# Down-projection of a ConvGLU layer: weight sums by accumulating DRAM transfers, activations put one combination at a time

## The chip, the cores and the metric

The kernel runs on one core of a Trainium2 chip. The metric is the device time of one execution in microseconds; the median of three runs of the kernel before is 2883.06 us (2882.86 to 2888.05). A profile is one further execution, taken by the hardware profiler.

In the profile PE is TensorE (products), PEld its weight loads, DVE is VectorE, ACT ScalarE, POOL GpSimd and SP the engine that only issues transfers. Each engine works through its own instructions in order; semaphores order the engines against each other.

## The reference

One layer of a streaming encoder, for 512 prompt frames and 64 sample frames: two recurrent mixers with their projections, then a ConvGLU feed-forward block, then a norm. What matters here is the feed-forward block (`D_MODEL` 2048, `D_FF` 5632, float32):

```python
def conv_ffn(h, st, w_up, ffn_conv_w, ffn_conv_b, w_down):
    gate, val = jnp.split(h @ w_up, 2, axis=-1)
    gate_c, new_st = causal_dwconv(gate, st, ffn_conv_w)
    act = jax.nn.silu(gate_c + ffn_conv_b) * val
    return act @ w_down, new_st
...
    f, s_f = conv_ffn(h, ffn_s[l], w_up[l], ffn_conv_w[l], ffn_conv_b[l], w_down[l])
    x = x + g2 * f
```

## The kernel before

**Products.** Frames stand on the free axis in two halves of 288 columns (256 prompt and 32 sample frames; 290 in the up-projection). Every float32 operand is split into a high and a low part (`hi` on ACT, `lo = x - hi` on DVE), and each product is three matmuls: hi by hi, hi by lo, lo by hi. Both projections of the feed-forward block use a fast two-by-two scheme with seven products in place of eight: the weight is cut into four blocks a11, a12, a21, a22, the activation into b11, b12, b21, b22, and the seven products (`c` = 0 to 6) take single blocks or sums of them, on both sides. The seven weights of a block are a11, s2 = s1 + a11, s1 = a21 + a22, a12, a11 + a21, s2 + a12 and a22.

**Up-projection** (`up`). 44 units `t`, each with seven products of 24 matmuls. `up_prep` runs two products ahead: it splits the weight of product `n + 2` into one of three buffers `wh`/`wl` (L1320, L1321), makes the weight sums on DVE (L1331 s1, L1340 s2, L1350, L1355) and issues the loads of the next unit's blocks (L1314, four of 512 KB, in SP's order a21, a22, a11, then two stores of the last unit's activation, then a12). There are six raw buffers, so a load waits until DVE has split what stood there. `up_out` takes the products out of three PSUM banks x, y and z; product `c` adds to bank x, y, z, x, y, z, y for c = 0 to 6. So y is read after c = 1, after c = 4 (L1396) and after c = 6, and each read stands between two products that write to it. At the end of a unit the gate goes into the convolution's buffer `cb` (L1409, L1410), POOL copies two columns into the new state `fs` (L1413, L1414), and in the next unit DVE convolves (L1423, `up_conv`), POOL puts the old state into `cb` (L1418, `up_state`), and the activation of the unit goes to DRAM (`actd`, L1431).

**Down-projection** (`down`). Activation tiles 0 and 1 (`FIRST`) are multiplied in the plain way first; the last four are left to `final`, which also norms and stores. The 38 between form 19 pairs `j`, in `GROUPS` of 3, 4, 4, 4 and 4 pairs; a group has four blocks `q` of output columns, and a block seven products. One product of a four-pair group has 24 matmuls, so a block has 168.

* *Weights.* Per block, `down_load` brings the four raw blocks (L1517, 512 KB each, 384 KB in the first group), `down_prep` makes four sums on DVE (`down_first` L1535, then L1552, L1562, L1567) and seven splits (L1541 on ACT, L1542 on DVE), two products ahead.
* *Activations.* `pair_load` brings both tiles of a pair into staging buffers, `down_pair` makes the seven combinations, each put into a slot as high and low part (L1224 on ACT, L1225 on DVE), with four differences on DVE (L1497, L1500, L1501, L1505). The four pairs of the next group are made at the products (q, c) = (2, 0), (3, 1), (3, 3) and (3, 5), a whole pair at a time. A slot is free once PE has done the last block's product with it.
* *Sums out.* `down_out` adds each product to accumulators in SBUF (L1607 from x and y, L1605 from z). x and y are two rotating PSUM tiles, so the next block's products wait for the sums out of the block before.
* *Staging.* Activation and residual loads share four buffers (`stage`: the convolution's `cb`, `ca` and two `v`), among them the loads of activations 0 and 1 at the start (L1478, split at L1484 and L1485).
* *End of a column block* (`down_finish`): load the residual `xd` (L1615), add `e0` (L1618), scale (L1622), add the residual (L1624).

The order on each engine comes from the program's order and a scheduler that may move an instruction ahead of others; `issue_after(ins)` keeps instructions behind `ins` on its engine.

Of the kernel before, what the change touches and what calls it, by code (L numbers as in the profile page):

```python
# [53 lines left out]
FIRST, NDOWN, GROUPS = 2, 19, (3, 4, 4, 4, 4)  # L54

# [46 lines left out]
class Kern:  # L102
# [530 lines left out]
    def raw_late(self):  # L633

        pool, tag = self.raws[self.n_raw % N_RAW]
        self.n_raw += 1
        return pool.tile([P, 1024], F32, tag=tag, name=self.name("raw"))
# [778 lines left out]
    def up_state(self, t):  # L1416

        self.nc.gpsimd.tensor_copy(self.cb[:, 514:516], self.vmap["st_ffn"].rearrange("p (i t) -> p t i", i=2)[:, t])  # L1418

# [18 lines left out]
    def up(self):  # L1438
# [49 lines left out]
    def pair_load(self, j):  # L1488
        return [self.act_load(FIRST + j + half * NDOWN) for half in range(2)]

    def down_pair(self, j, raws):

        V = self.nc.vector
        (b11, b12), (b21, b22) = [(r[:, 0], r[:, 1]) for r in raws]
        put = lambda c, b: self.put(c, j, b, None, HT)
        put(B11, b11)
        V.tensor_tensor(b11, b11, b12, op=ALU.subtract)  # L1497
# [4 lines left out]
        put(T2, b12)  # L1502
        put(T3, t)
        put(B21, b21)
        V.scalar_tensor_tensor(b21, b12, -1.0, b21, op0=ALU.mult, op1=ALU.subtract)  # L1505
        put(B22, b22)
        put(T4, b21)

# [11 lines left out]
    def down_load(self, step, names):  # L1520
        g, q = step
        for n in names:
            row, half = {"a11": (0, 0), "a12": (0, 1), "a21": (1, 0), "a22": (1, 1)}[n]
            k0, k1 = self.down_rows(g, half)
            m = (8 * row + 2 * q) * P
            self.a[g, q, n] = self.down_raw(self.i["w_down"][0, k0 * P:k1 * P, m:m + 256].rearrange("(k p) n -> p k n", p=P))

    def down_sum(self, step, c):
        g, q = step
        n = GROUPS[g]  # L1530
        return self.ua.tile([P, 1024], F32, tag=f"s{c}", name=self.name("s"))[:, :n * 256].rearrange("p (k n) -> p k n", k=n)

    def down_first(self, step):
        s1 = self.a[(*step, "s1")] = self.down_sum(step, 1)
        self.nc.vector.tensor_tensor(s1, self.a[(*step, "a21")], self.a[(*step, "a22")], op=ALU.add)  # L1535
# [9 lines left out]
    def down_prep(self, step, c, following):  # L1545

        V, a = self.nc.vector, self.a
        g = lambda n: a[(*step, n)]
        if c == 0:
            w = self.down_split(g("a11"))  # L1550
            s2 = a[(*step, "s2")] = self.down_sum(step, 2)
            V.tensor_tensor(s2, g("s1"), g("a11"), op=ALU.add)  # L1552
        elif c == 1:
            w = self.down_split(g("s2"))
        elif c == 2:
            w = self.down_split(g("s1"))
            if following:
                self.down_load(following, ("a21", "a22"))
        elif c == 3:
            w = self.down_split(g("a12"))  # L1560
        elif c == 4:
            V.tensor_tensor(g("a21"), g("a11"), g("a21"), op=ALU.add)  # L1562
            w = self.down_split(g("a21"))
            if following:
                self.down_load(following, ("a11", "a12"))
        elif c == 5:
            V.tensor_tensor(g("s2"), g("a12"), g("s2"), op=ALU.add)  # L1567
            w = self.down_split(g("s2"))
        else:
            w = self.down_split(g("a22"))  # L1570
            if following:
                self.down_first(following)
        a[(*step, "w", c)] = w
# [35 lines left out]
    def down_finish(self, row, h, q):  # L1609

        nc, t = self.nc, self.acc[row, h][q]
        xt = self.stage()
# [3 lines left out]
        if row + h:  # L1616
            yield
            nc.vector.tensor_tensor(t, t, self.e0[q], op=ALU.add)  # L1618
# [7 lines left out]
    def down(self):  # L1626
# [5 lines left out]
        self.places = firsts = take(2 * FIRST)  # L1632
        firsts = list(firsts)
        acts = [self.act_split(self.act_load(k)) for k in range(FIRST)]
# [8 lines left out]
        self.places += free + firsts  # L1643
# [5 lines left out]
        blocks = [b for b, c in steps if c == 0] + [None]  # L1649
        prep = lambda n: self.down_prep(*steps[n], blocks[n // 7 + 1]) if n < len(steps) else None  # L1650
        raws = {0: self.pair_load(0)}
        for m0 in range(0, KD, 4):
            wh, wl = self.wtile(self.i["w_down"][0, :FIRST * P, m0 * P:(m0 + 4) * P].rearrange("(k p) n -> p k n", p=P))
            if m0 == 4:
                self.down_load(blocks[0], ("a21", "a22"))
            if m0 == 8:
                self.down_load(blocks[0], ("a11", "a12"))
                self.down_first(blocks[0])
# [8 lines left out]
            if j < GROUPS[0]:  # L1667
                raws[j + 1] = self.pair_load(j + 1)
                self.down_pair(j, raws.pop(j))
        for n in range(2):  # L1670
            prep(n)

        j, last, tasks = GROUPS[0], len(GROUPS) - 1, []
        acts, loads = [], list(range(NFF - 4, NFF))
        for n, (step, c) in enumerate(steps):
            g, q = step
            prep(n + 2)
            self.down_product(step, c)
            self.down_out(step, c)
            if q == 3:  # L1680
                self.places += [self.combos[c, sum(GROUPS[:g]) + i][2] for i in range(GROUPS[g])]
            if g < last and (q, c) in ((2, 0), (3, 1), (3, 3), (3, 5)):
                if j + 1 < NDOWN:
                    raws[j + 1] = self.pair_load(j + 1)
                self.down_pair(j, raws.pop(j))
                j += 1
            if g == last:
                if q == 0 and c < 4:
                    loads[c] = self.act_load(loads[c])
                if q == 0 and 1 < c < 6:  # L1690
                    acts.append(self.act_split(loads[c - 2]))
                if c > 2:
                    tasks.append(self.down_finish(*((0, 0), (1, 1), (0, 1), (1, 0))[c - 3], q))
                for t in tasks[:2]:
                    if next(t, self) is self:
                        tasks.remove(t)
        for t in tasks:
            for _ in t:
                pass
# [111 lines left out]
def layer_kernel(tc, i, o):  # L1811
    nc = tc.nc
    with ExitStack() as ctx:
# [14 lines left out]
        K.actd = [dp.tile([P, 2, HT], F32, name=f"actd{t}") for t in range(NFF)]  # L1828
        K.hp = pool(ctx, "hp", bufs=1)
# [138 lines left out]
```

## Time and profile before

| | us |
|---|---|
| median of three runs | 2883.06 |
| the profiled execution's own time | 2889.4 |
| its span, first to last instruction | 2887.6 |
| up-projection, last unit ends at about | 2331 |
| down-projection with the final part, about | 2331 to 2888 |

A row of the windows gives, for a stretch of the span, the busy time of each engine with its number of instructions, the clock that TensorE was granted (1.00 is full speed), the share of time in which the 16 DMA engines were busy, and what they moved. A row of the waits reads: engine, line and tile that waited, what it waited for, total us, times, longest. A row of the groups gives line, engine, operation, tiles and shapes, then the total busy time, the mean of one in ns, and the idle time ahead of them with what ended it. "PE g" or "PE bank" are matmuls into a PSUM tile of that name; L561 and L563 are the plain products of the kernel's helper `mm6`, L1373 to L1375 those of the up-projection, L1590 to L1592 those of the down-projection.

### The profile page before, as it was taken

The numbers are of one execution on the slowest core, as the hardware profiler recorded it, in microseconds if no ns is written. First come the engines' busy times: TensorE is split into PE (matmuls) and PEld (weight loads), VectorE is DVE, ScalarE is ACT, GpSimd is POOL, SyncE is SP. The second block draws the span as 40 slices with busy tenths as digits, with TensorE's granted clock in tenths as the row PEclk, the third lists the DMA queues.
The fourth block names the chain that finished last, engine by engine and source line by source line (L and its number), as shares of the span: only waits on it lengthen the run. The fifth ranks groups of instructions, "written<-read, shape, count | busy, mean of one in ns | idle before, by whom it ended". The sixth has DMA issues, their size and how long they took to land.

```text
span 2887.6 us, 52030 instructions
## 1 busy us (share of the span) xinstructions
PE 2814.7 (97%) x20596; PEld 2713.3 (94%) x20596; DVE 2304.2 (80%) x3742; ACT 1357.9 (47%) x2379; POOL 320.9 (11%) x587
## 2 busy tenths in 40 slices
PE   7999999999999999999999999999999989999998
PEld 3599999999999999999999999999999989999997
DVE  5788888777778787468887888888888879999995
ACT  7574566544333333255444444444444454434453
POOL 0005432233310001001000000000000000000000
PEclk9999999999999999999999999999999999999999
DMA  9875555555456449333333333333333344333451
GB/s 306 298 205 155 156 146 161 157 142 157 128 158 183 136 136 260 111 112 97 104 105 111 101 108 107 101 101 107 110 102 108 108 131 121 120 112 121 129 160 66
DMA packets 523465, 399.80 MB, mean 138 GB/s; under 512 B 50793, under 2 KB 456004, under 8 KB 523220
## 3 DMA queue, kind: packets, MB, share of 16 engines
q1 hardware_dynamic: 517796, 385.79, 45.4%
q0 software_dynamic: 5424, 10.68, 1.2%
q8 instruction: 162, 2.65, 0.4%
q14 instruction: 83, 0.68, 0.1%
HBM read 356.24 MB, written 40.13 MB: 137 GB/s over the span
## 4 chain that ended last, share of the span: by engine, by line
PE 84%; DVE 7%; DMA 4%; ACT 3%; issue 1%; SPq 0%; POOL 0%; ACTq 0%; DVEq 0%; POOLq 0%
PE g L561 18%; PE g L563 9%; PE g L1373 9%; PE g L1374 8%; PE g L1375 8%; PE bank L1374 3%; PE bank L1373 3%; PE bank L1375 3%; PE g L1590 3%; PE g L1592 3%; PE g L1591 3%; DVE acc L820 1%; PE bank L1592 1%; PE bank L162 1%; PE bank L1590 1%
## 5 line engine op out<-in xcount | busy, mean ns | idle before, releaser
L1373 PE MATMUL g<-slot,wh 128*128 128x290 f32 x1760 | 533.2, 303 | 2.7 <-ACT p L1385 2.7
L1374 PE MATMUL g<-slot,wh 128*128 128x290 f32 x1760 | 525.9, 299 | 0.0
L1375 PE MATMUL g<-slot,wl 128*128 128x290 f32 x1760 | 520.2, 296 | 0.0
L561 PE MATMUL g<-hh,wh 128*128 128x288 f32 x1984 | 450.0, 306 | 1.0 <-DVE gcb L989 1.0
L561 PE MATMUL g<-hl,wh 128*128 128x288 f32 x1984 | 432.1, 297 | 0.0
L563 PE MATMUL g<-hh,wl 128*128 128x288 f32 x1984 | 432.0, 298 | 0.0
L1320 ACT ACTIVATE wh<-raw 128x1024 fp32r<-128x1024 f32 x176 | 186.7, 1061 | 396.0 <-PE g L1374 391.7
L1373 PEld LDWEIGHTS g<-slot,wh 128*128 128x128 f32 x1760 | 331.1, 188 | 17.0 <-ACT p L1385 11.6
L1375 PEld LDWEIGHTS g<-slot,wl 128*128 128x128 f32 x1760 | 336.3, 191 | 0.0
L1374 PEld LDWEIGHTS g<-slot,wh 128*128 128x128 f32 x1760 | 334.8, 190 | 0.1
L561 PEld LDWEIGHTS g<-hh,wh 128*128 128x128 f32 x1984 | 319.1, 190 | 4.0 <-DVE gcb L989 1.2
L561 PEld LDWEIGHTS g<-hl,wh 128*128 128x128 f32 x1984 | 321.1, 189 | 0.3
L649 ACT ACTIVATE wh<-raw 128x1024 fp32r<-128x1024 f32 x163 | 172.6, 1059 | 315.5 <-PE g L561 278.6
L563 PEld LDWEIGHTS g<-hh,wl 128*128 128x128 f32 x1984 | 320.0, 189 | 0.2 <-issue 0.2
L650 DVE TENSOR_TENSOR wl<-raw,wh 128x1024 fp32r<-128x1024 f32 x163 | 198.9, 1222 | 55.2 <-ACT wh L649 53.5
L820 DVE SCALAR_TENSOR_TENSOR acc<-xr,ct,acc 128x512 f32<-128x512 f32 x322 | 230.0, 749 | 2.2 <-DMA xr<-in_w_ada_dram 2.2
L1590 PE MATMUL g<-slot,wh 128*128 128x288 f32 x760 | 225.4, 297 | 6.5 <-DVE slot L1607 6.5
L1321 DVE TENSOR_TENSOR wl<-raw,wh 128x1024 fp32r<-128x1024 f32 x176 | 214.7, 1220 | 18.8 <-ACT wh L1320 18.7
L1592 PE MATMUL g<-slot,wl 128*128 128x288 f32 x760 | 224.7, 296 | 0.0
L1591 PE MATMUL g<-slot,wh 128*128 128x288 f32 x760 | 224.5, 295 | 0.0
L1374 PE MATMUL bank<-slot,wh 128*128 128x290 f32 x704 | 210.1, 298 | 0.0
L1373 PE MATMUL bank<-slot,wh 128*128 128x290 f32 x704 | 209.4, 297 | 0.0
(410 smaller groups left out, 6085.0 us busy)
## 6 DMA issues: line engine op xcount, KB each, us to landing
raw<-in_w_up_dram SPq DMA_DIRECT2D x176, 512.0 KB, 4.1
raw<-in_w_in_dram SPq DMA_DIRECT2D x108, 512.0 KB, 4.0
xr<-in_w_ada_dram SPq DMA_DIRECT2D x86, 512.0 KB, 3.8
raw<-in_w_down_dram SPq DMA_DIRECT2D x76, 512.0 KB, 3.6
ax<-in_w_ada_dram SPq DMA_DIRECT2D x42, 512.0 KB, 3.9
hraw<-in_w_ada_dram SPq DMA_DIRECT2D x40, 512.0 KB, 9.1
raw<-in_w_out_dram SPq DMA_DIRECT2D x32, 512.0 KB, 4.3
raw<-actd SPq DMA_DIRECT2D x44, 288.0 KB, 3.2
```

What stands on the lines that cost most here:

```text
L561: T.matmul(ps[:, h if bank is None else bank, :n], wh, x[:, h, :n], start=f, stop=False)
L563: T.matmul(ps[:, h if bank is None else bank, :n], wl, ah[:, h, :n], start=False, stop=stop)
L650: nc.vector.tensor_tensor(lo[:, :n_], raw[:, :n_], hi[:, :n_].bitcast(F32), op=ALU.subtract)
L820: V.scalar_tensor_tensor(acc[s], w[:, k], col, acc[s], op0=ALU.mult, op1=ALU.add)
L1320: self.nc.scalar.activation(hi, src, AF.Copy)
L1321: self.nc.vector.tensor_tensor(lo, src, hi.bitcast(F32), op=ALU.subtract)
L1373: T.matmul(ps, wh[:, j], hi, start=(c < 3 and j == 0), stop=False, skip_group_check=True)
L1374: T.matmul(ps, wh[:, j], lo, start=False, stop=False, skip_group_check=True)
L1375: T.matmul(ps, wl[:, j], hi, start=False, stop=(j == NPAIR - 1), skip_group_check=True)
L1590: T.matmul(ps, wh[:, j, f], hi, start=(c < 3 and j == 0), stop=False, skip_group_check=True)
L1591: T.matmul(ps, wh[:, j, f], lo, start=False, stop=False, skip_group_check=True)
L1592: T.matmul(ps, wl[:, j, f], hi, start=False, stop=(j == n - 1), skip_group_check=True)
```

## The change

**Weight sums.** The four sums that a block needs become four arrays in DRAM per group, `ws[g]`: s1 = a21 + a22, s2 = s1 + a11, s3 = a11 + a21, s4 = s2 + a12, for all 1024 output columns at once. Each is made by POOL's transfers: a copy from DRAM to DRAM, then a transfer that adds to what stands there (`accum_op=add`). There are ten pieces (two tile rows of a group, or one, 1 MB or 0.5 MB) and eight transfers a piece, 80 in all, in two batches of five pieces, so that a transfer builds on the one five places back. `up` draws two of them in each unit, at c = 1 and c = 4, behind the copy of the old state (`issue_after(self.state_of)`). `down_load` then loads the weight of each product, a block of `w_down` or of `ws`, seven for a block in place of four, four products ahead of its split (`RAW_AHEAD`); the two buffers of the DVE sums join the raw buffers, eight in all. `down_prep` is left with the load and the split.

**Activations.** `down_pair` becomes a generator that yields after each put. `next_pairs` goes through the pairs of the next group; the loop draws one put in each product of block 2 and 0, 3, 4, 4, 3, 4, 3 in those of block 3. Activations 0 and 1 and the first group's pairs are loaded into free slots instead of staging buffers.

**End.** The steps of `down_finish` stand at fixed products (`events`): for the four accumulators of a column block the load at products 1 to 4, the scaling two products later and the residual one after that. The additions of `e0` stand at products 1 to 3. The last four activations are loaded and split one for each block of the last group.

```diff
+RAW_AHEAD = 4
...
     def up_state(self, t):
 
         self.nc.gpsimd.tensor_copy(self.cb[:, 514:516], self.vmap["st_ffn"].rearrange("p (i t) -> p t i", i=2)[:, t])
+        self.state_of = self.nc.cur_bb.bb.instructions[-1]
...
+        sums = self.down_sums()
         for n, (t, c) in enumerate(steps):
+            if c in (1, 4):
+                with self.tc.issue_after(self.state_of):
+                    next(sums, None)
...
-    def act_load(self, t):
-
-        raw = self.stage()
+    def act_load(self, t, place=None):
+
+        raw = self.slot(place, F32, HT) if place else self.stage()
         self.nc.sync.dma_start(raw, self.actd[t])
...
+    def next_pairs(self, pairs):
+
+        raws = [self.pair_load(pairs[0])]
+        yield
+        for n, j in enumerate(pairs):
+            if n + 1 < len(pairs):
+                raws.append(self.pair_load(pairs[n + 1]))
+            yield from self.down_pair(j, raws.pop(0))
...
+    def down_sums(self):
+
+        dma, add = self.nc.gpsimd.dma_start, ALU.add
+        pieces = [(g, k) for g in range(len(GROUPS)) for k in range(0, GROUPS[g], 2)]
+        for batch in (pieces[:5], pieces[5:]):
+            for op in range(8):
+                for g, k in batch:
+                    rows = slice(k * P, min(k + 2, GROUPS[g]) * P)
+                    a11, a12, a21, a22 = [self.down_block(g, *at)[rows] for at in ((0, 0), (0, 1), (1, 0), (1, 1))]
+                    s1, s2, s3, s4 = [w[rows] for w in self.ws[g]]
+                    to, of = ((s1, a21), (s1, a22), (s2, s1), (s2, a11), (s3, a11), (s3, a21), (s4, s2), (s4, a12))[op]
+                    if op % 2:
+                        dma(to, of, accum_op=add)
+                    else:
+                        dma(to, of)
+                    yield
+
+    def down_load(self, step, c):
         g, q = step
...
+        s1, s2, s3, s4 = self.ws[g]
+        src = (self.down_block(g, 0, 0), s2, s1, self.down_block(g, 0, 1), s3, s4, self.down_block(g, 1, 1))[c]
+        self.a[g, q, c] = self.down_raw(src[:, 2 * q * P:2 * (q + 1) * P].rearrange("(k p) n -> p k n", p=P))
...
-    def down_prep(self, step, c, following):
-
-        V, a = self.nc.vector, self.a
-        g = lambda n: a[(*step, n)]
-        if c == 0:
-            w = self.down_split(g("a11"))
-            s2 = a[(*step, "s2")] = self.down_sum(step, 2)
-            V.tensor_tensor(s2, g("s1"), g("a11"), op=ALU.add)
...
+    def down_prep(self, n):
+
+        steps = self.steps
+        if n + RAW_AHEAD < len(steps):
+            self.down_load(*steps[n + RAW_AHEAD])
+        if n < len(steps):
+            step, c = steps[n]
+            self.a[(*step, "w", c)] = self.down_split(self.a.pop((*step, c)))
...
+        self.raws += [(self.ua, "s1"), (self.ua, "s2")]
+        firsts = take(3 * FIRST)
+        loads = [self.act_load(k, firsts[k]) for k in range(FIRST)]
...
+        puts = {2: (1,) * 7, 3: (0, 3, 4, 4, 3, 4, 3)}
...
+        for q in range(4):
+            b = 7 * (4 * last + q)
+            for i, (row, h) in enumerate(((0, 0), (1, 1), (0, 1), (1, 0))):
+                f = self.down_finish(row, h, q)
+                for at in (1, 3, 4):
+                    events[b + i + at].append(lambda f=f: next(f, None))
...
-            if g < last and (q, c) in ((2, 0), (3, 1), (3, 3), (3, 5)):
-                if j + 1 < NDOWN:
-                    raws[j + 1] = self.pair_load(j + 1)
-                self.down_pair(j, raws.pop(j))
-                j += 1
...
+                for _ in range(puts[q][c] if q in puts else 0):
+                    next(pairs)
```

Where the instructions stand, at three places. First POOL in the middle of the up-projection, before: the two copies into `fs` and the copy of the old state into `cb`, unit after unit.

```order
L1413 COPY fs<-cb 128x2
L1414 COPY fs<-cb 128x2
L1418 COPY cb<-cols 128x2
L1413 COPY fs<-cb 128x2
L1414 COPY fs<-cb 128x2
```

The same place of the changed kernel. `ws` is an array of sums; L1561 is a copy, L1559 a transfer that adds; 16x16384 is a whole piece of another sum.

```order
L1419 COPY cb<-cols 128x2
L1561 DMA ws_186<-ws_185 16x16384
L1559 DMA ws_178<-in_w_down_dram 256x1024
L1414 COPY fs<-cb 128x2
L1415 COPY fs<-cb 128x2
L1419 COPY cb<-cols 128x2
```

Both transfers of a unit stand back to back behind the copy of the state, and ahead of the next unit's copies into `fs`.

Second ACT at the way from the up- to the down-projection, before: L1320 and L649 are weight splits (of the last unit, and of the plain products), L1409 to L1424 the last unit's gate and convolution, L1484 the splits of activations 0 and 1, L1224 puts.

```order
L1320 ACTIVATE wh_25433<-s_25267 128x1024
L1320 ACTIVATE wh_25462<-raw_25098 128x1024
L649 ACTIVATE wh_25597<-raw_25596 128x1024
L649 ACTIVATE wh_25693<-raw_25692 128x1024
L1484 ACTIVATE slot_25565<-raw_25563 128x576
L1409 ACTIVATE cb<-g_25395 128x512
L1410 ACTIVATE cb<-g_25395 128x64
L649 ACTIVATE wh_25793<-raw_25792 128x1024
L1412 ACTIVATE ca_25520<-cb,cols 128x578
L1424 ACTIVATE ca_25520<-ca_25520,cols 128x578
L1484 ACTIVATE slot_25559<-raw_25557 128x576
```

The same place of the changed kernel (L1321 and L650 are the weight splits, L1490 the splits of activations 0 and 1, L1386 and L1426 belong to the last two units):

```order
L1321 ACTIVATE wh_25431<-s_25335 128x1024
L1490 ACTIVATE slot_25661<-slot_25657 128x576
L1386 ACTIVATE p_3327_25465<-g_25435 128x290
L1321 ACTIVATE wh_25467<-raw_25269 128x1024
L1426 ACTIVATE ca_25397<-ca_25397,cols 128x578
L1490 ACTIVATE slot_25665<-slot_25659 128x576
L1321 ACTIVATE wh_25498<-raw_25196 128x1024
L1321 ACTIVATE wh_25533<-s_25367 128x1024
L1321 ACTIVATE wh_25562<-raw_25198 128x1024
L650 ACTIVATE wh_25705<-raw_25704 128x1024
```

Both splits moved from around the last convolution to ahead of the last unit's weight splits.

Third DVE at the end of the first group, before: L1542 are lo-splits of weights, L1605 and L1607 sums out of PSUM, L1225 puts, L1497, L1501 and L1505 differences of activations.

```order
L1605 TENSOR_TENSOR slot_25576<-bank_26554,slot_25576 128x288
L1225 TENSOR_TENSOR slot_26765<-raw_26680,slot_26765 128x288
L1225 TENSOR_TENSOR slot_26778<-t_3564_26772,slot_26778 128x288
L1497 TENSOR_TENSOR raw_26680<-raw_26680 128x288
L1225 TENSOR_TENSOR slot_26781<-raw_26682,slot_26781 128x288
L1501 SCALAR_TENSOR_TENSOR raw_26680<-raw_26680,raw_26682 128x288
L1225 TENSOR_TENSOR slot_26769<-raw_26680,slot_26769 128x288
L1505 SCALAR_TENSOR_TENSOR raw_26682<-raw_26680,raw_26682 128x288
L1225 TENSOR_TENSOR slot_26785<-raw_26682,slot_26785 128x288
L1542 TENSOR_TENSOR wl_26792<-s_26739,wh_26791 128x1024
```

The same place of the changed kernel (L1575 are lo-splits, L1617 and L1619 sums out, L1226 puts, L1509 and L1515 differences):

```order
L1617 TENSOR_TENSOR slot_25676<-bank_26652,slot_25676 128x288
L1226 TENSOR_TENSOR slot_26863<-raw_26778,slot_26863 128x288
L1509 SCALAR_TENSOR_TENSOR raw_26778<-raw_26778,raw_26780 128x288
L1575 TENSOR_TENSOR wl_26878<-raw_26714,wh_26877 128x1024
L1226 TENSOR_TENSOR slot_26869<-raw_26778,slot_26869 128x288
L1619 TENSOR_TENSOR slot_25680<-g_26650,slot_25680 128x576
L1515 SCALAR_TENSOR_TENSOR raw_26780<-raw_26778,raw_26780 128x288
L1226 TENSOR_TENSOR slot_26904<-raw_26780,slot_26904 128x288
L1575 TENSOR_TENSOR wl_26913<-raw_26753,wh_26912 128x1024
```

Five puts in a row became one or two between a lo-split and a sum out, and the lo-splits read raw loads where they read a DVE sum (`s`).

More of the change, by code (lines that the diff above doesn't have):

```diff
@@ L1687, in down @@
[L1687 to L1699, printed above, removed]
+            freed = lambda c: [self.combos[c, sum(GROUPS[:g]) + i][2] for i in range(GROUPS[g])]
@@ new lines, in down @@
+            if q == 3 and c > 0:
+                self.places += freed(c - 1)
+            if g < last:
+                if (q, c) == (1, 6):
+                    pairs = self.next_pairs(range(sum(GROUPS[:g + 1]), sum(GROUPS[:g + 2])))
+                    next(pairs)
+                for _ in range(puts[q][c] if q in puts else 0):
+                    next(pairs)
+            for f in events[n]:
+                f()
+            if q == 3 and c == 6:
+                next(pairs, None)
+                self.places += freed(c)
```

101 lines of the change are left out of this document (39 added, 62 removed).

## The prediction

> **What bounds the kernel now.** I read the page's first four parts, then the windows by stage, then the waits of the stage that changes, then one unit of the up-projection in order of time.
>
> ```profile
> PE 2814.7 (97%) x20596; PEld 2713.3 (94%) x20596; DVE 2304.2 (80%) x3742; ACT 1357.9 (47%) x2379; POOL 320.9 (11%) x587
> PE   7999999999999999999999999999999989999998
> PE 84%; DVE 7%; DMA 4%; ACT 3%; issue 1%; SPq 0%; POOL 0%; ACTq 0%; DVEq 0%; POOLq 0%
> ```
>
> TensorE is the bound. The change leaves the number of products as it is, so it can only take away, or add, time in which PE waits or runs at a lower clock.
>
> ```profile
> 1300.00:2300.00 1000.00, 996.88 (x7271) 982.23 (x7270) 819.01 (x1024) 451.73 (x548) 71.02 (x133) 1.00 0.36 105
> 2320.00:2400.00 80.00, 70.36 (x511) 69.59 (x510) 66.30 (x119) 45.41 (x97) 1.09 (x2) 0.94 0.45 135
> 2400.00:2800.00 400.00, 393.29 (x2948) 391.91 (x2948) 380.90 (x533) 187.46 (x284) 0.00 (x0) 1.00 0.43 127
> 2540.00:2620.00 80.00, 80.00 (x605) 80.00 (x605) 76.81 (x110) 34.28 (x46) 0.00 (x0) 1.00 0.40 122
> 2640.00:2660.00 20.00, 20.00 (x154) 20.00 (x153) 19.58 (x28) 7.48 (x9) 0.00 (x0) 1.00 0.31 97
> 2800.00:2820.00 20.00, 14.17 (x92) 13.87 (x91) 17.40 (x34) 9.37 (x22) 0.00 (x0) 0.83 0.43 135
> ```
>
> Columns: window, length, busy time and count of PE, PEld, DVE, ACT, POOL, granted clock, DMA share, GB/s. The first row is the up-projection: PE has 3 us of gaps in 1000, DMA stands at 0.36. The others are the down-projection. In its clean stretch (2540 to 2620) PE does 605 products in 80 us, 7.56 per us; DVE is 95% busy over 2400 to 2800.
>
> **What the change can take from the down-projection.** Products missing against the clean rate: (605 - 511) / 7.56 = 12.4 us at the way in; (5 x 605 - 2948) / 7.56 = 10.2 us in the 400 us of groups; (154 - 92) / 7.56 = 8.2 us where the final part begins. That is 30.8 us, the ceiling. Their causes, PE's waits from 2300 on:
>
> ```profile
> PE g L561 <- ACT slot L1484: 8.9, 1, 8.9
> PE g L1590 <- DVE slot L1607: 6.5, 5, 1.9
> PE bank L1787 <- DVE slot L1714: 5.8, 1, 5.8
> ```
>
> *Way in.* 8.9 us, the rest is the lower clock (0.94) after it. Activation 0 is loaded into a buffer that the last unit's convolution holds. The change loads it into slots that PE leaves with the last unit's first product, and the order on ACT has both splits (L1490 there) among that unit's weight splits. What is late next is the first weight split, which stands there already; I let 1 us stand: gain 11.
>
> *Groups.* DVE is late with its sums out of PSUM when a group changes. What it loses:
>
> ```profile
> L1542 DVE TENSOR_TENSOR wl<-raw,wh 128x1024 fp32r<-128x1024 f32 x64 | 78.0, 1218 | 0.6 <-ACT wh L1541 0.2
> L1607 DVE TENSOR_TENSOR slot<-g,slot 128x576 f32<-128x576 f32 x96 | 72.3, 753 | 4.1 <-PE g L1592 3.8
> L1225 DVE TENSOR_TENSOR slot<-raw,slot 128x288 fp32r<-128x288 f32 x114 | 49.6, 454 | 4.7 <-ACT slot L1224 4.7
> L1605 DVE TENSOR_TENSOR slot<-bank,slot 128x288 f32<-128x288 f32 x80 | 34.5, 452 | 5.1 <-PE bank L1592 4.8
> L1552 DVE TENSOR_TENSOR s<-s,raw 128x1024 f32<-128x1024 f32 x16 | 19.5, 1221 | 1.6 <-DMA raw<-in_w_down_dram 1.4
> L1562 DVE TENSOR_TENSOR raw<-raw,raw 128x1024 f32<-128x1024 f32 x16 | 19.5, 1218 | 0.0
> L1497 DVE TENSOR_TENSOR raw<-raw 128x288 f32<-128x288 f32 x19 | 8.6, 455 | 0.1
> ```
>
> DVE loses the four sums of each block (L1552 and L1562 are two of them): in 16 blocks of four tiles 64 x 1.22 = 78 us of some 450 us, and shorter ones in the four blocks of three tiles, so that it goes from 95% to about 77%. The last block of a group still holds seven lo-splits (7 x 1.22 = 8.5 us), its sums out (5 x 0.75 + 4 x 0.45 = 5.6), 21 puts (L1225) and 12 differences (L1497) at 0.45 (15): 29 us of DVE beside 168 products, 22.2 us. So DVE still falls behind there, but it now enters the block on time, has 4.9 us less to do in it than before, and its puts stand between the sums out instead of in three lumps. I take 8.5 of the 10.2 us; all or none of them are the bounds.
>
> *Final part.* The residual loads move two steps forward and no longer wait for a buffer at the end; the scaling and adding behind the last product stay. Of 8.2 us I take 5; bounds 0 and 8. Sum of the gains: **25 us**, between 11 and 31. The 60 more weight loads (seven for four in 20 blocks, 0.5 MB) add 30 MB to 450 us, 67 GB/s on 127; with four steps of 24 products (12.7 us) of lead they are covered by PE's own work; without it each load would cost the 4 us that it takes to land. The e0 additions and the residual's instructions only change places.
>
> **What it adds to the up-projection.** 80 transfers of up to 1 MB, DRAM to DRAM, two a unit. Order shows them back to back behind the copy of the state. What stands there (POOL, SP, DVE, PE in one unit; a unit is 900 us / 39 = 23 us by the last row):
>
> ```profile
> 1808.69 1.05 POOL L1418 COPY cb<-cols 128x2 f32<-128x2 f32 x1 [6.12 <-DVE ca L1423]
> ```
> ```profile
> 1809.72 0.37 SPq L1314 DMA_DIRECT2D raw<-in_w_up_dram  x1
> ...
> 1813.66 0.37 SPq L1314 DMA_DIRECT2D raw<-in_w_up_dram  x1
> ```
> ```profile
> 1818.10 1.23 DVE L1340 TENSOR_TENSOR s<-s,raw 128x1024 f32<-128x1024 f32 x1 [1.10 <-DMA raw<-in_w_up_dram]
> 1819.24 1.22 DVE L1321 TENSOR_TENSOR wl<-raw,wh 128x1024 fp32r<-128x1024 f32 x1
> 1820.38 1.22 DVE L1350 TENSOR_TENSOR raw<-raw,raw 128x1024 f32<-128x1024 f32 x1
> 1821.51 0.45 DVE L1396 TENSOR_TENSOR v<-g,r 128x290 f32<-128x290 f32 x1
> ```
> ```profile
> 1822.95 0.30 PE L1373 MATMUL g<-slot,wh 128*128 128x290 f32 x1
> ```
> ```profile
> DVE s L1340 <- DMA raw<-in_w_up_dram: 48.7, 39, 1.6
> ```
>
> The load issued at 1813.66 (a11 of the next unit, the one ahead of the two stores) is the only late one: DVE waits for it in each of 39 units. Behind that wait, in order, DVE has two weight operations and L1396, which reads the bank that PE's last product of the unit adds to. L1396 ends at 1821.96, that product starts at 1822.95: **slack 0.99 us**. Anything that delays this load by more stops PE, once a unit.
>
> ```profile
> 1814.50:1815.00 0.50, 0.50 (x6) 0.50 (x5) 0.50 (x2) 0.00 (x0) 0.00 (x0) 1.00 0.25 70
> 1817.00:1817.50 0.50, 0.50 (x5) 0.44 (x4) 0.00 (x1) 0.47 (x1) 0.00 (x0) 1.00 1.09 359
> 1817.50:1818.00 0.50, 0.50 (x6) 0.50 (x5) 0.00 (x0) 0.00 (x0) 0.00 (x0) 1.00 0.48 109
> ```
> ```profile
> q1 hardware_dynamic: 182917, 93.83, 36.3%
> ```
>
> No row shows a transfer inside DRAM, so I bound it by these. The load's bytes move from about 1814.5 to 1817.7; 359 GB/s is the most that 0.5 us shows. The new pair starts after the copy, with an issue and a start as long as the load's own: about 1810.7. Until 1814.5 the engines can move 3.8 x 359 = 1.36 MB, of which 0.52 MB is the load of 1809.72; of the pair's 2.10 MB, 1.26 are left. With those ahead of it, the load (0.52 MB) and the stores (0.29 MB) end 2.07 MB / 359 = 5.8 us later, at 1820.3: delay 2.6 us, PE stops for 2.6 - 0.99 = 1.6 us. I count the pair's bytes once. Over 40 units: **64 us**. Lower bound: the two queues share the time in halves; then 0.81 MB at 180 GB/s take 4.6 us, the delay is 1.4, the stop 0.4, 16 us in all; and 0 if a transfer inside DRAM hardly loads the engines. Upper bound: an accumulation costs twice. Units come as 16 of two copies, 8 mixed, 16 of two accumulations; their stops are 1.6, 4.5 and 7.4 us, together 180 us. I take 64, since it is what the measured rate gives without a factor that no row shows.
>
> By the Trainium skill (DMA: Bandwidth & Descriptors, section Queues, rings and completion order) an engine goes round its queues a packet at a time. The q1 row has 93.83 MB in 182917 packets, 513 bytes each, and a row of the new transfers is 4 KB; under that rule the pair goes ahead, not in halves, so it gives the 64 us and not the 16. No run here has tried it.
>
> POOL itself has cover: it idles 6.12 us ahead of the state copy in the first row, so two issues hide. The change adds waits there: a transfer waits for the one eight back, and an accumulation for the one five back that it builds on, 2.5 units earlier. Behind them stand the copies into fs and the next state copy, for which DVE's convolution (and then all that follows on DVE) would wait; at one pair in 10 us nothing waits. No instruction of the up-projection on another engine moves, and the last transfer is issued four units ahead of the first use.
>
> **Sum.** 2889.4 (the profiled execution's own time, span 2887.6) - 25 + 64 = 2928. That execution is 6.3 us above the median of 2883.06, so 2922 for the median.
>
> **Rivals.**
> *Hidden.* The transfers leave the a11 load within its 0.99 us, since DMA is idle 64% of the up-projection. For it: every other load has slack (the one of 1809.72 is used a unit later). Against it: the burst starts 4 us ahead of the one load without slack. It decides at a delay of 0.99 us. Time: 2889.4 - 25 - 6.3 = 2858; with shared halves 2874. Faster.
> *Accumulations cost double.* 2889.4 - 25 + 180 - 6.3 = 3038. For it: the target must be read as well as written; against it, only that no row shows it. By the Trainium skill (Collectives: The Full Stack, section The bandwidth ceiling: the fold count and why AG ≠ RS ≠ AR) a reducing transfer reads two sources and runs at about half a copy's rate; that rule would give this time.
> *The queue fills.* The loads take 0.363 x 23 = 8.3 us of a unit, so 14.7 are left. If a pair takes longer, transfers pile up, POOL waits for the one five or eight back, and the state copy and the convolution behind it hold the unit: over 3040.
> *It does not relieve DVE.* If the puts alone keep the groups' waits, 8.5 us of gain go: about 2930, inside the forecast's range.
>
> **How the numbers follow.** Forecast (stops of 0.8 to 2.5 us a unit, 2890 to 2965) 0.42; hidden 0.28; cancelling (stop of about 0.6 us, within 5.8 us of no change) 0.08; double 0.15; queue 0.07. About 0.2% is what a measurement of this kernel can tell from no change. Faster 0.28, same 0.08, slower 0.64. The range goes from the hidden case's 2858, less 2, to 3010, into the double case; the queue case, most of the double one's upper half and a little below are left out.
>
> **What would show it.** Right: in some 40 units PE waits for DVE at the unit's last product (for the add that is L1396 before), DVE's wait for the load of w_up grows from 1.2 to near 4 us, that load lands 6 to 7 us after its issue, and a unit takes some 24.6 us instead of 23. The double case shows units of about 30 us in groups of two; hidden shows 23 us throughout. In the down-projection the waits of 8.9 and 6.5 us should be gone and DVE near 77%. The prediction is wrong if that load's landing does not move, or if PE stops at another product.

## The result and the profile after

| | before | after |
|---|---|---|
| median of the runs taken together, us | 2885.21 (4 runs) | 3167.8 (4 runs, 3163.1 to 3169.24) |
| ratio | 1 | 1.0976, 95% interval 1.0957 to 1.0995 |
| span of the profiled execution, us | 2887.6 | 3161.3 |

The change makes the kernel 9.8% slower. The forecast had the direction, at 2922 us, but the time lies far above its range. Of all executions told of here one, of run 4 below, was in a slower state (3395.91 us at a granted clock of 0.75); no ratio includes it, and without it run 4's median is 2880.2 us.

The page of the changed kernel: busy time of each engine, then PE and its granted clock in 40 slices, then the chain that ended last.

```profile
PE 2888.5 (91%) x20596; PEld 2780.5 (88%) x20596; DVE 2226.8 (70%) x3662; ACT 1356.9 (43%) x2379; POOL 370.3 (12%) x667
...
PE   7999999999999999988888888888788799999998
...
PEclk9999999999999999988998988888888899999999
...
PE 68%; DMA 16%; DVE 9%; ACT 4%; issue 2%; SPq 0%; POOL 0%; ACTq 0%; DVEq 0%; POOLq 0%
```

The same 20596 products take 2888.5 us of PE instead of 2814.7, and PE is now idle for 9% of a longer span. In the chain, DMA's share has grown from 4% to 16%. Against the kernel before, both rows of digits fall in one stretch alone, the up-projection. One window over it, from the first to the last product of line L1373 (L1374 after), for the kernel before:

```profile
1313.00:2332.00 1019.00, 1015.88 (x7406) 1000.77 (x7405) 834.27 (x1041) 458.08 (x551) 70.12 (x132) 1.00 0.37 105
```

and for the changed kernel:

```profile
1310.60:2629.40 1318.80, 1096.37 (x7406) 1073.46 (x7405) 834.68 (x1041) 459.27 (x555) 119.33 (x214) 0.90 0.54 143
```

The stretch is 299.8 us longer. PE's busy time for the same 7406 products grows by 80.5 us, at a granted clock of 0.90; the gaps between products grow from 3.1 to 222.4 us. The span grew by only 273.7, so everything else became 26.1 us **shorter**: 23.7 of them behind the up-projection (555.6 us became 531.9), which is the gain in the down-projection, and 2.4 ahead of it, in a part that the change leaves alone. PE's waits in the changed kernel from 1300 on, with the one load that DVE waits for:

```profile
DVE s L1341 <- DMA raw<-in_w_up_dram: 300.2, 42, 10.9
...
PE g L1374 <- DVE v L1397: 213.4, 37, 8.8
...
PE bank L1805 <- DVE slot L1732: 2.0, 1, 2.0
...
PE g L562 <- ACT slot L1672: 1.2, 1, 1.2
```

This is the stop that the prediction described, at the place that it named: DVE waits for a11 of the next unit (L1341, before L1340), the add L1397 (before L1396) comes late, and PE waits for it. Its size is another: 10.9 us at most, not 4. The waits of 8.9 us at the way into the down-projection and of 6.5 us at its group changes are gone, and the one of 5.8 us in the final part is 2.0 (L1805). The down-projection, in three windows:

```profile
2629.40:2700.00 70.60, 69.37 (x521) 68.94 (x521) 57.17 (x106) 43.64 (x95) 0.00 (x0) 1.00 0.58 180
2700.00:3000.00 300.00, 300.00 (x2267) 300.00 (x2266) 241.87 (x373) 136.79 (x195) 0.00 (x0) 1.00 0.63 197
3000.00:3161.00 161.00, 145.43 (x1086) 142.66 (x1084) 117.73 (x213) 78.10 (x164) 3.23 (x6) 0.96 0.48 147
```

In the middle one PE has no gap in 300 us (2267 products, 7.56 per us, the clean rate); DVE is 81% busy.

**One unit.** A unit whose two transfers are both accumulations, on POOL, then DVE, then PE:

```profile
2199.17 1.05 POOL L1419 COPY cb<-cols 128x2 f32<-128x2 f32 x1 [7.27 <-DVE ca L1425]
2200.17 1.78 POOL L1559 DMA_DIRECT2D ws<-in_w_down_dram  x2
...
2232.69 1.05 POOL L1419 COPY cb<-cols 128x2 f32<-128x2 f32 x1 [7.76 <-DVE ca L1425]
```
```profile
2217.77 1.23 DVE L1341 TENSOR_TENSOR s<-s,raw 128x1024 f32<-128x1024 f32 x1 [10.12 <-DMA raw<-in_w_up_dram]
```
```profile
2221.78 0.58 PE L1374 MATMUL g<-slot,wh 128*128 128x290 f32 x1 [7.99 <-DVE v L1397]
```

From state copy to state copy the unit takes 33.5 us instead of 23. PE stops for 7.99 us. Windows of the same unit, and the transfers' own queue in the first of them:

```profile
2201.50:2217.50 16.00, 12.29 (x91) 11.94 (x89) 4.50 (x7) 3.19 (x3) 0.45 (x1) 0.97 0.99 214
2214.00:2221.50 7.50, 0.00 (x0) 0.00 (x0) 3.73 (x4) 2.11 (x2) 0.00 (x0) 0.68 0.46 123
2221.50:2226.50 5.00, 4.71 (x19) 4.75 (x20) 4.46 (x6) 1.74 (x3) 0.42 (x2) 0.50 0.69 205
```
```profile
q0 software_dynamic: 544, 2.10, 68.9%
```

Three things are to be seen. All 16 DMA engines are full for 16 us (share 0.99), and yet only 214 GB/s move. The pair's 2.10 MB take 68.9% of that, 11.0 us. And when PE starts again, the granted clock is 0.50: 19 products in 5 us, where the clean rate gives 38.

The Trainium skill has a rule for this last row (TensorE: Matmul & The Clock Gate, section Part 1: The HAM clock gate): after about 3.4 us of idling the array's clock drops to half, and it needs about as long of steady work to come back. The trace agrees in part: the clock is at half behind a stop of 7.99 us, but for some 5 us, and run 2 shows the low clock behind a stop of 3.16 us too.

Not every unit stops as long. PE stops for 3.2 us at the mean in the 16 units of two copies (two of these stops, of 1.1 us, and the 6.3 us of the first unit end on other instructions than L1397), for 6.4 in the 8 mixed ones and for 7.4 in the 16 of two accumulations. Four of these last have one transfer of half size and stop for 5.1 us; the other twelve stop for 8.2.

### The profile page after: what moved, and what is told of

It reads as the page before. It is cut to its first block, busy times and chain, and to the rows that moved or that the text cites. A ratio compares the mean times of both kernels' runs of the same rounds, so it can differ in the third digit from the quotient of the medians.

```text
span 3161.3 us, 52279 instructions
## 1 busy us (share of the span) xinstructions
PE 2888.5 (91%) x20596; PEld 2780.5 (88%) x20596; DVE 2226.8 (70%) x3662; ACT 1356.9 (43%) x2379; POOL 370.3 (12%) x667
## 3 DMA queue, kind: packets, MB, share of 16 engines
q0 software_dynamic: 21616, 90.37, 11.4%
## 4 chain that ended last, share of the span: by engine, by line
PE 68%; DMA 16%; DVE 9%; ACT 4%; issue 2%; SPq 0%; POOL 0%; ACTq 0%; DVEq 0%; POOLq 0%
PE g L562 17%; DMA raw<-in_w_up_dram 13%; PE g L564 8%; PE g L1374 6%; PE g L1375 6%; PE g L1376 5%; PE g L1604 3%; PE g L1603 3%; PE g L1602 3%; DVE wl L1322 3%; ACT wh L1321 1%; DVE raw L1351 1%; PE bank L1602 1%; PE bank L1604 1%; PE bank L1603 1%
## 5 line engine op out<-in xcount | busy, mean ns | idle before, releaser
L1374 PE MATMUL g<-slot,wh 128*128 128x290 f32 x1760 | 572.2, 325 | 222.0 <-DVE v L1397 213.4
L1374 PEld LDWEIGHTS g<-slot,wh 128*128 128x128 f32 x1760 | 364.1, 207 | 244.3 <-issue 219.2
L1375 PE MATMUL g<-slot,wh 128*128 128x290 f32 x1760 | 557.9, 317 | 0.0
L1376 PE MATMUL g<-slot,wl 128*128 128x290 f32 x1760 | 551.7, 313 | 0.0
L1321 ACT ACTIVATE wh<-raw 128x1024 fp32r<-128x1024 f32 x176 | 186.6, 1060 | 560.6 <-PE g L1375 282.6
L1375 PEld LDWEIGHTS g<-slot,wh 128*128 128x128 f32 x1760 | 367.7, 209 | 0.1
L1376 PEld LDWEIGHTS g<-slot,wl 128*128 128x128 f32 x1760 | 367.7, 209 | 0.0
L650 ACT ACTIVATE wh<-raw 128x1024 fp32r<-128x1024 f32 x163 | 172.6, 1059 | 311.9 <-PE g L562 276.9
L1341 DVE TENSOR_TENSOR s<-s,raw 128x1024 f32<-128x1024 f32 x44 | 53.9, 1226 | 301.1 <-DMA raw<-in_w_up_dram 301.1
L1574 ACT ACTIVATE wh<-raw 128x1024 fp32r<-128x1024 f32 (+1 forms) x140 | 142.2, 1015 | 180.9 <-PE g L1603 107.1
## 6 DMA issues: line engine op xcount, KB each, us to landing
ws<-in_w_down_dram POOLq DMA_DIRECT2D x54, 1024.0 KB, 11.6
```

What stands on the lines that cost most here:

```text
L1321: self.nc.scalar.activation(hi, src, AF.Copy)
L1374: T.matmul(ps, wh[:, j], hi, start=(c < 3 and j == 0), stop=False, skip_group_check=True)
L1375: T.matmul(ps, wh[:, j], lo, start=False, stop=False, skip_group_check=True)
L1376: T.matmul(ps, wl[:, j], hi, start=False, stop=(j == NPAIR - 1), skip_group_check=True)
```

## The experiments

Theories on record: the burst of transfers collides with the one load that has no slack (A), against a general excess of bytes, wherever they stand (B); and for the size, what an accumulation costs beside a copy.

**1. The down-projection alone.** No transfers; blocks of w_down are loaded in place of the sums.

```diff
-        sums = self.down_sums()
+        sums = iter(())
...
-        src = (self.down_block(g, 0, 0), s2, s1, self.down_block(g, 0, 1), s3, s4, self.down_block(g, 1, 1))[c]
+        src = self.down_block(g, *((0, 0), (1, 0), (1, 1), (0, 1), (1, 0), (0, 1), (1, 1))[c])
```

> This kernel issues none of the 80 sum transfers; the down-projection loads plain blocks of w_down in place of the sums (as many loads of the same size), so those products are of other numbers and the output is not the reference's. Theory A (the forecast's ledger for the down-projection holds, and the whole loss lies in the up-projection): 25 us less than before, 2860 us, within 2852 to 2874 (11 to 31 us less), no wait of DVE for a load of w_up above 2 us, granted clock 0.99 or more. Rival (part of the loss lies in the new down-projection): over 2885 us.

Measured: 2862.43 us beside 2884.67 before, ratio 0.9924 (0.991 to 0.9939). The up-projection in one window:

```profile
1315.00:2332.30 1017.30, 1014.01 (x7406) 999.07 (x7405) 835.34 (x1039) 459.07 (x553) 72.59 (x134) 1.00 0.37 107
```

A gain of 22.2 us by the medians. By the profiles it is 2887.6 - 2861.7 = 25.9, of which the up-projection accounts for 1.7; the part ahead of it happens to be 2.0 longer, so 26.2 stand behind it (555.6 us became 529.4). Theory A of this run held (2852 to 2874 us); the whole loss comes from the transfers.

**2. The same transfers without adding.** The order of DVE's instructions is that of the changed kernel.

```diff
-                        dma(to, of, accum_op=add)
+                        dma(to, of)
```

> All 80 transfers stay where they are with the same bytes, but none accumulates: each is a plain copy, so the sums and the output are not the reference's. Theory A (an accumulation holds the queues for about twice the time of a copy, so the burst delays the late load twice as long): units with two transfers of the second kind fall from 33.5 us to the 25 to 28 us of the units that copy between scratch blocks or the 25 to 31 us of those that copy from w_down; 40 units that stop about 4 us each, less 25 us in the down-projection, 2990 to 3050 us. Rival (the stop comes from the number of transfers or of bytes written, whichever kind they are): 3150 to 3170 us, units unchanged.

Measured: 3066.29 us, ratio 1.0625 (1.0598 to 1.0653), against 1.0976 with accumulation. So a third of the loss is the adding, and two thirds come with plain copies: 204 us more than in run 1, above the range expected (2990 to 3050 us). The up-projection, then one unit of two copies (all transfers, then PE's stop, then what follows it), the queue of the transfers in the first of these, and the late load:

```profile
1314.90:2538.80 1223.90, 1090.22 (x7406) 1067.22 (x7405) 833.93 (x1041) 458.96 (x555) 105.21 (x214) 0.93 0.50 154
```
```profile
1911.50:1922.70 11.20, 11.20 (x84) 11.08 (x84) 4.50 (x7) 3.18 (x3) 0.00 (x0) 1.00 0.93 304
1923.50:1926.80 3.30, 0.48 (x4) 0.25 (x2) 3.30 (x4) 1.76 (x2) 0.00 (x0) 1.00 0.03 8
1927.00:1931.50 4.50, 4.35 (x21) 4.38 (x22) 4.32 (x5) 1.74 (x3) 0.42 (x2) 0.62 0.78 223
```
```profile
q0 software_dynamic: 544, 2.10, 52.3%
```
```profile
1923.13 1.23 DVE L1341 TENSOR_TENSOR s<-s,raw 128x1024 f32<-128x1024 f32 x1 [5.27 <-DMA raw<-in_w_up_dram]
```

A pair of copies takes 52.3% of 11.2 us of the engines, 5.9 us for 2.10 MB; a pair of accumulations took 11.0 us for as many bytes, **1.9 times as long**. The profiles' pages say the same of all 80 transfers: their queue q0 takes 11.4% of the span in the changed kernel and 8.4% here, for 90.37 MB in both; less the 1.2% of the kernel before that is 326 us against 223. As only half of the transfers accumulate, an accumulation costs 1.9 copies there too. And even a stop of 3.16 us is followed by a low clock (0.62 over 4.5 us). Over the stretch the copies lose 133.7 - 3.1 = 130.6 us in gaps and 1090.22 - 1015.88 = 74.3 us in clock; accumulating adds 89 us of gaps and only 6 of clock. That is about 1.9 to 2.0 us of clock for each of 40 units. Stop by stop, over the traces of the changed kernel and of runs 2, 3 and 5, no stop of 0.7 to 1.7 us is followed by a low clock and each one above 2.5 us is; behind the latter the half clock lasts some 3 to 6 us, and little longer for stops of 8 us than for stops of 4. Behind a stop of 1.08 us in the changed kernel, for one:

```profile
1790.50:1800.00 9.50, 9.01 (x65) 8.84 (x66) 9.40 (x12) 4.47 (x7) 0.42 (x2) 1.00 0.38 111
```

**3. Slack for the late load.** All transfers stay. In the up-projection a21 - a11 is formed earlier, which frees a11's buffer for the next unit's a11.

```diff
         elif c == 1:
             w = self.up_split(g("s2"))
+            V.tensor_tensor(g("a21"), g("a11"), g("a21"), op=ALU.subtract)
         elif c == 2:
...
-                self.up_load(t + 1, ("a21", "a22"))
+                self.up_load(t + 1, ("a11", "a21", "a22"))
         elif c == 4:
-            V.tensor_tensor(g("a21"), g("a11"), g("a21"), op=ALU.subtract)
             w = self.up_split(g("a21"))
-            if t + 1 < NFF:
-                self.up_load(t + 1, ("a11", "a12"))
         elif c == 5:
...
+            if t + 1 < NFF:
+                self.up_load(t + 1, ("a12",))
```

(and `up_load` takes fixed buffers: one for a11, one for a12, two each for a21 and a22.)

> The changed kernel with one thing more: in the up-projection a21 is replaced by a11 - a21 two steps after a11 is first read instead of four, so that a11's buffer is free at once; a11 of the next unit goes into it and is issued some 15 us before it is needed instead of 5. The transfers stay as they are. Theory A (the stop is a collision of the burst with the one load that has 1 us of slack): the units return to about 23 us, DVE's wait for loads of w_up falls from 300 us to under 30 us, time 2855 to 2880 us. Theory B (the loads and the transfers together are too much for the queues or the memory, wherever each stands): units stay near 30 us, since every unit still has to bring the same bytes; time 3100 us or more.

(The difference is formed one step after a11 is first read, not two as this says.)

Measured: **2873.82 us**, ratio 0.9962 (0.9947 to 0.9977), inside theory A's 2855 to 2880. The up-projection, and DVE's wait for loads of w_up:

```profile
1307.40:2339.20 1031.80, 1017.47 (x7406) 1002.65 (x7405) 833.53 (x1039) 458.36 (x553) 146.57 (x213) 0.99 0.70 183
```
```profile
DVE s L1333 <- DMA raw<-in_w_up_dram: 22.9, 13, 4.3
```

The same bytes now move in 1031.8 us instead of 1318.8, at 183 GB/s instead of 143 and a clock of 0.99. Theory B is refuted; nearly all of the loss was one load without slack. It also shows that the low clock came from the stops and not from the transfers, which are all still there. Some 14 us stay, 5 of them in the first unit.

**4. The same slack in the kernel before.** The same edit of the up-projection, nothing else of the change.

> The kernel before, with the earlier load of a11 alone and no other part of the change. Theory A: in the kernel before nothing in the up-projection ended on that load, so the time stays at 2885 us within 5 us; what the kernel with both gains is then not due to the earlier load by itself. Rival (the earlier load is a gain of its own): 2870 us or less.

Measured: 2881.51 us, ratio 0.9987 (0.9977 to 0.9997). At most a small gain of its own; it gives back nothing in the kernel before, since nothing there ended on that load. So the gain of run 3 is not one that the new order on DVE brings by itself.

**5. The two transfers of a unit apart.** DVE's order is again that of the changed kernel.

```diff
-            if c in (1, 4):
-                with self.tc.issue_after(self.state_of):
+            if c in (1, 6):
+                with self.tc.issue_after(self.state_of if c == 1 else self.gate_of):
```

(`gate_of` is the second copy into fs.)

> The changed kernel with the two transfers of a unit issued apart: one still behind the copy of the state, the other behind the copies into fs, some 7 us earlier in the unit. Same 80 transfers, same sums. Theory A (only what is in the engines when the a11 load is issued delays it): a lone copy (about 3 us of all 16 engines by the run without accumulation, 2.10 MB in 20.2% of 29 us) delays it by about 1 us and stops nothing; a lone accumulation (about 5.5 us, 2.10 MB in 73.5% of 15 us) stops PE by about 3 us and costs 2 us of clock; 20 x 5 + 20 x 0.5 + 2862 + the first burst's 5 = 2975 us, within 2940 to 3010. Theory B (the bytes of a unit count, not their place): 3150 us or more.

Measured: 2961.25 us, ratio 1.0253 (1.0234 to 1.0271), inside theory A's 2940 to 3010. PE's wait of 213.4 us falls to:

```profile
PE g L1374 <- DVE v L1397: 60.1, 31, 4.9
```

Two thirds of the loss go by issuing one of two transfers some 7 us earlier, with every byte still in the same unit. What stands in the engines when the load is issued is what counts.

**6. Pieces of 512 bytes.**

```diff
+                    to, of = [w.rearrange("r (a b) -> a r b", b=P) for w in (to, of)]
```

> The changed kernel with each transfer walked in columns of 128 numbers, so that it goes as pieces of 512 bytes, as the loads of w_up do, instead of about 4 KB; the same sums. Theory A (an engine takes its queues in turn, a packet at a time, so that the load gets a share by packets): the load of a11 now gets about half of the engines while it is there, takes about 5 us instead of 13, and PE stops under 1.5 us a unit: 2880 to 2930 us. Theory B (the pair goes first whatever its pieces, or small pieces cost the engines more): 3150 us or more, and transfers that take longer than the 10.3 us at the median that they take in the changed kernel.

Measured: 3292.74 us, ratio 1.1409 (1.139 to 1.1428), above theory B's 3150. The transfers' queue over 1310 to 2700, one kind of transfer with its median time to landing, and two waits:

```profile
q0 software_dynamic: 176384, 80.63, 35.0%
...
ws<-in_w_down_dram POOLq DMA_DIRECT2D x54, 1024.0 KB, 20.0
```
```profile
PE g L1374 <- DVE g L1389: 167.6, 39, 9.6
DVE s L1341 <- DMA raw<-in_w_up_dram: 164.8, 41, 9.0
```

The transfers land after 20.0 us instead of 11.6. But DVE's order in the up-projection differs here too, and PE now waits for another instruction (L1389), so this run says that the kernel is slower with small pieces and that these land later, and nothing certain on how queues share an engine. In the changed kernel the pair goes first, or nearly: the load lands when the pair is done. Why is open; that an engine changes queues by the pieces that the profile counts, as the prediction assumed, is not shown.

**7. Sums put back on DVE.** The kernel of run 1 with four additions a block (of a tile to itself) in the down-projection.

```diff
+            if c in (1, 2, 4, 5):
+                self.nc.vector.tensor_tensor(raw, raw, raw, op=ALU.add)
```

> The kernel without the transfers and without the sums (plain blocks of w_down, output not the reference's), with four additions of 128 x 1024 a block put back on DVE in the down-projection, as many as DVE's sums were before; they add a tile to itself. Everything else of the new down-projection stays: puts one at a time, early loads of the activations. Theory A (DVE's relief is what takes the waits at the group changes away, 8.5 us in the forecast): 2868 to 2875 us and DVE waited for at the group changes again. Rival (the puts one at a time do it, and the sums in DRAM buy nothing): 2862 us within 3.

Measured: 2870.5 us, ratio 0.9946 (0.9933 to 0.996), against 0.9924 (0.991 to 0.9939) without them. The intervals overlap, but each of the five executions is slower than each of the four of run 1, and the medians differ by 8.1 us. So DVE's relief is worth some 8 us, and the larger part of the gain, about two thirds, comes from the puts one at a time and the earlier loads, which need no sums in DRAM. The groups in these two kernels, run 7 first:

```profile
2400.00:2780.00 380.00, 377.63 (x2839) 376.18 (x2839) 365.09 (x517) 179.84 (x273) 0.00 (x0) 1.00 0.66 199
...
2402.00:2782.00 380.00, 380.00 (x2871) 380.00 (x2870) 310.85 (x463) 187.08 (x289) 0.00 (x0) 1.00 0.67 203
```

With the sums back DVE is 96% busy and 32 products are missing, 4.2 us; the rest falls at the way in and in the final part. PE's waits at the sums out stay small even so:

```profile
PE g L1605 <- DVE slot L1622: 2.3, 2, 1.2
```

**8. A version that beats both.** Run 3, with a21 and a22 ahead of a11 in the load order, and the transfers begun two units later.

```diff
-                self.up_load(t + 1, ("a11", "a21", "a22"))
+                self.up_load(t + 1, ("a21", "a22", "a11"))
...
-            if c in (1, 4):
+            if c in (1, 4) and t > 1:
```

> The kernel with the earlier load of a11, and two things more: a21 and a22 are issued ahead of a11 (they are used first now), and the first pair of transfers stands two units later. Theory A: the first unit loses its 5 us of burst, and the 2 us or so that every second pair of accumulations still cost go in part: 2862 to 2870 us, faster than the kernel before at 2885. Theory B (some loss stays with the bytes): 2874 us as with the earlier load alone.

Measured: **2869.22 us** beside 2886.33 before, ratio 0.9933 (0.9916 to 0.995); it is faster than the kernel before by 17 us and computes the whole reference. Its up-projection takes as long as before the change (1018.8 us beside 1019.0). Run 3 had 0.9962 (0.9947 to 0.9977), so the intervals touch, and which of the two small edits did it was not tried apart. PE's waits for DVE over the up-projection's units are now:

```profile
PE g L1375 <- DVE g L1395: 1.4, 5, 0.3
```

## Why the prediction was wrong

**The gains: right in sum.** 25 us were forecast; behind the up-projection the profiles of the changed kernel and of run 1 give 23.7 and 26.2. *Way in:* the window from 2629.4 misses 7.56 x 70.6 - 521 = 13 products, 1.7 us; 1 us was forecast to stay. *Groups:* no gap is left where 1.7 us were to stay; DVE does not fall behind in the last block of a group. But by run 7 only some 4 of the 10 us that the groups lost are owed to DVE's relief; the puts one at a time and the earlier loads are worth the larger part there too; the prediction named both causes and left their shares open. *Final part:* of the 23.7 us some 3 are left for it, where 5 were forecast. *DVE near 77%:* 81%.

**The place of the loss: right.** a11, L1341, L1397, the unit's last product, once a unit; runs 3 and 5 show that it is the cause, and not only the place where the wait is seen. The clean time of 23 us stays in units without transfers. The wait for the eighth and fifth transfer back stopped nothing in the changed kernel, so the rival of the full queue fell as well, though the time lies above its 3040. "Hidden" fell in this kernel; run 8, which gives the load its slack, comes within 11 us of its 2858.

**The size: wrong.** The step that failed is the term "64 us", 40 stops of 1.6 us: "I count the pair's bytes once", at 359 GB/s, "without a factor that no row shows". That the late load stops PE was right; three sizes in the term were not. The term first, then the sizes that the runs put in their place:

| | forecast | measured |
|---|---|---|
| PE's stops in 40 units | 64 us | 219.3 us more gaps (222.4 - 3.1) |
| rate of all engines, pair of copies and loads together | 359 GB/s | 304 GB/s (run 2) |
| an accumulation beside a copy | 1.0 | 1.9 (11.0 us beside 5.9) |
| clock lost behind a stop | nothing | about 2 us a unit, 80.5 us in all |

*The rate.* The pair, two loads and the stores are 2.10 + 2 x 0.52 + 0.29 = 3.43 MB: 9.6 us at 359 GB/s, 11.3 at 304, so 1.7 us more delay. The most that half a microsecond had shown was taken for what a burst holds. The two copies themselves do move at that rate (2.10 MB in 5.9 us); the loads and stores beside them do not. The prediction's own q1 row has 93.83 MB in 36.3% of 900 us, 287 GB/s with all engines busy, and the 359 were read in a row whose DMA share is 1.09. The stop behind two copies is 3.2 us at the mean, twice the forecast.

*The accumulation.* The rival "double" named this factor, with its reason, and it is the mechanism that came out: its stop of 7.4 us for two accumulations is the mean of the 16 such units (the mixed ones stop for 6.4 us where it had 4.5). That the figure is met so closely is in part luck: the twelve with two whole transfers stop for 8.2 us and four with a half one for 5.1, while the prediction counted 2.10 MB in every unit and the higher rate. It was given a chance of 0.15 because no row showed it. The factor lay between 1 and 2, with a reason for 2 in the prediction and none for 1, and was settled at 1.

*The clock.* Neither the forecast nor that rival has this term, though the prediction used the very thing for the way in ("the rest is the lower clock (0.94) after it"). Stops of 180 us by the rival and 80 us of clock, less 25 of gain, are 3118 for the median; up to 1.7 us a unit for the lower rate make it 3186 at most. The measured 3167.8 lies between; this sum was made after the runs and is no test of them.

By the Trainium skill (Collectives: The Full Stack, section The bandwidth ceiling: the fold count and why AG ≠ RS ≠ AR) a reducing transfer runs at about half a copy's rate; the page gives this for collectives in a ring of cores. The rows of run 2 and of the changed kernel agree, with 1.9 for transfers inside DRAM.

## What to carry to other kernels

Before transfers are added behind an engine that has room, find the load that is issued last before it is needed, and give it slack first: here one buffer freed three products earlier turned a loss of 283 us into a gain of 11. Price a burst by the rate that a long stretch of the same mix holds (bytes by the time that their packets took, over many units), not by the best half microsecond, and an accumulating transfer at twice a copy until a row shows otherwise. Where PE stops in every unit, add the slow clock behind each stop to the stop itself: here about 2 us for each stop above 2.5 us. And take apart what a change bundles: two thirds of the gain here need no transfers at all.

## What the runs showed of the hardware

Accumulating transfers inside DRAM, with the loads beside them, fill the DMA engines while they move 214 GB/s, where copies and loads together move 304; an accumulation takes 1.9 times the engines' time of a copy. The granted clock falls to 0.50 behind a stop of 8 us, and already behind one of 3.16 us it averages 0.62 over the next 4.5 us; behind one of 1.08 us it stays at 1.00. The time lost so is nearly the same for stops of copies and of accumulations (74.3 and 80.5 us in 40 units). Transfers in pieces of 512 bytes instead of 4 KB take 20.0 us to land instead of 11.6.
